# The first load of a row-mean kernel, issued as two transfers: partitions 0 to 15, then 16 to 127

## The chip, the cores and the metric

One core of one Trainium2 chip. The time is the device time of the core in microseconds (us), as a median over several executions.

Some terms: data comes from HBM (67.11 MB read, by the page of before) into SBUF, where a tile of this kernel has 128 partitions (128x14336 in the reductions). DMA engines move it: the packet records of before fall into sixteen strings, taken here as one per engine. A packet is one such record, here the rows of one load for one partition (57,344 B for 14 rows). A transfer is issued by one instruction and has landed when all its packets are written.

## The reference

```python
batch, seq, dim = 32, 512, 1024
def reference(x, divisor):           # x: (32, 512, 1024) float32, divisor 1024.0
    return (np.sum(x, axis=-1) / divisor).astype(np.float32)
```

There are 16,384 rows of 4 KB, 67.1 MB in all, each summed to one number. The work is to read everything once.

## The kernel before

Each of the 128 partitions gets 128 rows. A load takes some rows of every partition; VectorE sums them with one reduction per load, ScalarE helps at the end. All loads go through one queue (issued by SyncE), into three large buffers of 14 rows, and the first three are issued before anything else runs.

```python
first = [(2, 0), (14, 0)]                            # (rows, of these on ScalarE)
main = [(14, 0)] * 5 + [(14, 4), (12, 5)]
last = [(9, 4), (4, 2), (2, 1)]
...
for loads, src, dst in ((first, x_first, res0), (main, x_main, res)):
    j = 0
    for rows, on_act in loads:
        t = bulk.tile([P, 14, D], F32, name="t")     # three buffers
        load(t[:, :rows, :], src[:, j : j + rows, :])
        d = rows - on_act
        ...                                          # ScalarE sums rows d to rows-1
        nc.vector.reduce_sum(out=dst[:, j : j + d], in_=t[:, :d, :], axis=AX)
        j += rows
    nc.gpsimd.tensor_scalar_mul(out=dst, in0=dst, scalar1=scale)
...                                                  # the last 16 rows, in ever smaller loads: t, t4, t2, pa, pb
```

Of the kernel before, what the change touches and what calls it, by code (L numbers as in the profile page):

```python
# [125 lines left out]
@with_exitstack  # L126
def kernel(
    ctx: ExitStack,
    tc: tile.TileContext,
    x: bass.AP,  # L130
    divisor: float,
    out: bass.AP,
):
    nc = tc.nc
    landed = nc.alloc_semaphore("landed")
    nc.at_finalize(start_loads_at_once)
    nc.at_finalize(latest_wait_first)
    nc.at_finalize(lambda nc: close_while_storing(nc, landed))
    xf = x.flatten_outer_dims()
    N, D = xf.shape  # L140
    P = nc.NUM_PARTITIONS
    scale = 1.0 / float(divisor)
    J = N // P
    assert J * P == N


    F, L = 16, 16
    M = J - F - L
    W = M + L
    x_first = bass.AP(tensor=x.tensor, offset=0, ap=[[F * D, P], [D, F], [1, D]])  # L150
    x_main = bass.AP(tensor=x.tensor, offset=P * F * D, ap=[[W * D, P], [D, M], [1, D]])
    x_last = bass.AP(tensor=x.tensor, offset=P * F * D + M * D, ap=[[W * D, P], [D, L], [1, D]])
    o_first = bass.AP(tensor=out.tensor, offset=0, ap=[[F, P], [1, F]])
    o_main = bass.AP(tensor=out.tensor, offset=P * F, ap=[[W, P], [1, M]])
    o_last = bass.AP(tensor=out.tensor, offset=P * F + M, ap=[[W, P], [1, L]])


    first = [(2, 0), (14, 0)]
    main = [(14, 0)] * 5 + [(14, 4), (12, 5)]
    last = [(9, 4), (4, 2), (2, 1)]  # L160
    assert sum(n for n, _ in first) == F
    assert sum(n for n, _ in main) == M and sum(n for n, _ in last) == L - 1

    pad = ctx.enter_context(tc.tile_pool(name="pad", bufs=1))
    pad.tile([P, 224], F32, name="pad")
    bulk = ctx.enter_context(tc.tile_pool(name="bulk", bufs=3))
    one = ctx.enter_context(tc.tile_pool(name="one", bufs=1))
    psum = ctx.enter_context(tc.tile_pool(name="junk", bufs=4, space=bass.MemoryType.PSUM))


    c = 512
    t4 = one.tile([P, 4, D], F32, name="t4")
    t2 = one.tile([P, 2, D], F32, name="t2")
    pa = one.tile([P, 768], F32, name="pa")[:, :c]
    pb = one.tile([P, D - c + 16], F32, name="pb")[:, : D - c + 2]
    res0 = one.tile([P, F], F32, name="res0")
    res = one.tile([P, M], F32, name="res")
    fin = one.tile([P, L], F32, name="fin")
    nc.gpsimd.memset(pb[:, D - c :], 0.0)  # L179

    def load(dst, src):
        tc.keep_in_program_order(nc.sync.dma_start(out=dst, in_=src))  # L182

    def act_sum(dst, src, by=1.0):
        junk = psum.tile([P, D], F32, name="junk")
        nc.scalar.activation(junk, src, COPY, scale=by, accum_out=dst)  # L186

    def dve_mean(dst, src, by=scale):


        h = src.shape[-1] // 2
        nc.vector.tensor_tensor_reduce(  # L192
            out=src[:, :h], in0=src[:, :h], in1=src[:, h:], scale=by, scalar=0.0,
            op0=ADD, op1=ADD, accum_out=dst,
        )

    for loads, src, dst in ((first, x_first, res0), (main, x_main, res)):
        j = 0
        for rows, on_act in loads:
            t = bulk.tile([P, 14, D], F32, name="t")  # L200
            load(t[:, :rows, :], src[:, j : j + rows, :])
            d = rows - on_act
            for i in range(d, rows):
                act_sum(dst[:, j + i : j + i + 1], t[:, i, :])
# [4 lines that stand above are left out]
    for rows, on_act in last:  # L209
        t = bulk.tile([P, 14, D], F32, name="t")[:, :rows, :] if rows > 4 else t4 if rows == 4 else t2  # L210
        load(t, x_last[:, j : j + rows, :])
        d = rows - on_act
        for i in range(rows):
            if i < d:
                dve_mean(fin[:, j + i : j + i + 1], t[:, i, :])
            else:
                act_sum(fin[:, j + i : j + i + 1], t[:, i, :], by=scale)
        j += rows
    load(pa, x_last[:, j, :c])
    load(pb[:, : D - c], x_last[:, j, c:])  # L220


    tc.keep_in_program_order(nc.sync.dma_start(out=o_first, in_=res0))
    tc.keep_in_program_order(nc.sync.dma_start(out=o_main, in_=res))

    dve_mean(pb[:, D - c : D - c + 1], pa, by=1.0)
    dve_mean(fin[:, j:], pb)
    tc.keep_in_program_order(nc.sync.dma_start(out=o_last, in_=fin))
# [35 lines left out]
```

## Time and profile before

| | before |
|---|---|
| time | 160.38 us, median of 3 (160.35 to 160.44) |
| span of the profile | 159.0 us |
| VectorE busy | 117.2 us |
| DMA, mean over the span | 422 GB/s |
| a 57,344 B packet (14 rows), start to start on one DMA engine | 2.113 us, 27.1 GB/s |
| an 8,192 B packet (the first load's 2 rows) | 0.306 us |
| first load landed, first reduction starts | 4.63 us |
| last load (pb) landed | 157.08 us |

The prediction below shows the lines and works them out.

### The profile page before, as it was taken

The numbers are of one execution on the slowest core, as the hardware profiler recorded it, in microseconds if no ns is written. First come the engines' busy times: TensorE is split into PE (matmuls) and PEld (weight loads), VectorE is DVE, ScalarE is ACT, GpSimd is POOL, SyncE is SP. The second block draws the span as 40 slices with busy tenths as digits, with TensorE's granted clock in tenths as the row PEclk, the third lists the DMA queues.
The fourth block names the chain that finished last, engine by engine and source line by source line (L and its number), as shares of the span: only waits on it lengthen the run. The fifth ranks groups of instructions, "written<-read, shape, count | busy, mean of one in ns | idle before, by whom it ended". The sixth has DMA issues, their size and how long they took to land.

```text
span 159.0 us, 148 instructions
## 1 busy us (share of the span) xinstructions
DVE 117.2 (74%) x29; ACT 18.5 (12%) x33; POOL 1.0 (1%) x7
## 2 busy tenths in 40 slices
DVE  0500059995999599978999599959995996395643
ACT  3000000000000000000000000000000900390684
POOL 0000000000000000000000000000000000001000
DMA  7999999959999999699999999699999999999894
GB/s 278 447 462 462 462 462 462 462 260 433 462 462 462 462 462 462 303 390 462 462 462 462 462 462 404 303 447 462 462 462 429 396 396 408 482 445 445 350 420 169
DMA packets 2448, 67.18 MB, mean 422 GB/s; under 512 B 656, under 2 KB 656, under 8 KB 912
## 3 DMA queue, kind: packets, MB, share of 16 engines
q1 hardware_dynamic: 2448, 67.18, 98.3%
HBM read 67.11 MB, written 0.07 MB: 422 GB/s over the span
## 4 chain that ended last, share of the span: by engine, by line
DMA 77%; DVE 21%; SPq 1%; issue 0%; DVEq 0%
DMA t<-in_x_dram 56%; DMA pb<-in_x_dram 21%; DVE res L205 20%; SPq L182 1%; DVE pb L192 0%; DVEq L259 0%
## 5 line engine op out<-in xcount | busy, mean ns | idle before, releaser
L205 DVE TENSOR_REDUCE res<-t 128x14 f32<-128x14336 f32 (+3 forms) x9 | 111.2, 12360 | 34.0 <-DMA t<-in_x_dram 34.0
L186 ACT ACTIVATE junk<-t 128x1024 f32<-128x1024 f32 x16 | 16.2, 1013 | 136.8 <-DMA t<-in_x_dram 136.8
L192 DVE CUSTOM_DVE_ANT_0 t<-t 128x512 f32<-128x512 f32 x8 | 5.1, 688 | 6.1 <-DMA t<-in_x_dram 6.1
L186 ACT ACTIVATION_READ_ACCUMULATOR junk<-t 128x1 f32 x16 | 3.0, 186 | 0.0
L207 POOL TENSOR_SCALAR res<-res 128x16 f32<-128x16 f32 (+1 forms) x2 | 0.7, 352 | 143.3 <-DVE res L205 143.3
L186 ACT ACT_TABLE_LOAD x1 | 1.3, 1283 | 1.7 <-PEq L245 1.7
L192 DVE DVE_READ_ACCUMULATOR2_ANT fin<- 128x1 f32 x9 | 0.7, 82 | 0.0
L192 DVE CUSTOM_DVE_ANT_0 pb<-pb 128x257 f32<-128x257 f32 x1 | 0.4, 428 | 0.2 <-DMA pb<-in_x_dram 0.2
L192 DVE CUSTOM_DVE_ANT_0 pa<-pa 128x256 f32<-128x256 f32 x1 | 0.4, 426 | 0.0
L179 POOL MEMSET pb<- 128x2 f32 x1 | 0.1, 99 | 1.3 <-POOLq L245 1.3
L245 POOL MEMSET const-bfloat16-1.0<- 128x1 bf16 x1 | 0.1, 101 | 0.0
L245 POOL MEMSET const-uint8-127<- 128x1 uint8 x1 | 0.1, 101 | 0.0
L245 POOL MEMSET const-float32-0.0<- 128x1 f32 x1 | 0.1, 98 | 0.2 <-issue 0.2
L245 POOL MEMSET const-float32-1.0<- 128x1 f32 x1 | 0.1, 98 | 0.0
L192 DVE DVE_READ_ACCUMULATOR2_ANT pb<- 128x1 f32 x1 | 0.1, 84 | 0.0
## 6 DMA issues: line engine op xcount, KB each, us to landing
t<-in_x_dram SPq DMA_DIRECT2D x7, 7168.0 KB, 35.6
t<-in_x_dram SPq DMA_DIRECT2D x1, 6144.0 KB, 33.3
t<-in_x_dram SPq DMA_DIRECT2D x1, 4608.0 KB, 27.2
t<-in_x_dram SPq DMA_DIRECT2D x2, 1024.0 KB, 19.2
t<-in_x_dram SPq DMA_DIRECT2D x1, 2048.0 KB, 31.7
pa<-in_x_dram SPq DMA_DIRECT2D x1, 256.0 KB, 33.8
pb<-in_x_dram SPq DMA_DIRECT2D x1, 256.0 KB, 33.9
out_dram<-res SPq DMA_DIRECT2D x1, 48.0 KB, 11.6
```

The source lines that it names most:

```text
L179: nc.gpsimd.memset(pb[:, D - c :], 0.0)
L182: tc.keep_in_program_order(nc.sync.dma_start(out=dst, in_=src))
L186: nc.scalar.activation(junk, src, COPY, scale=by, accum_out=dst)
L192: nc.vector.tensor_tensor_reduce(out=src[:, :h], in0=src[:, :h], in1=src[:, h:], scale=by, scalar=0.0, op0=ADD, op1=ADD, accum_out=dst,)
L205: nc.vector.reduce_sum(out=dst[:, j : j + d], in_=t[:, :d, :], axis=AX)
L207: nc.gpsimd.tensor_scalar_mul(out=dst, in0=dst, scalar1=scale)
L245: nc = _bacc.Bacc("TRN2", target_bir_lowering=False, num_devices=1)
```

## The change

The intent is to give every DMA engine its first packet sooner: the first issue covers only 16 partitions, one row pair for each of the 16 engines, and the other 112 partitions follow.

```diff
         for rows, on_act in loads:
             t = bulk.tile([P, 14, D], F32, name="t")
-            load(t[:, :rows, :], src[:, j : j + rows, :])
+            if rows == 2:
+
+                load(t[:16, :rows, :], src[:16, j : j + rows, :])
+                load(t[16:, :rows, :], src[16:, j : j + rows, :])
+            else:
+                load(t[:, :rows, :], src[:, j : j + rows, :])
```

## The prediction

> **What bounds the kernel now.** I read the page's first two parts, then the chain of waits, the waits of the load queue, the order in time of the first microseconds, and at last the trace's single DMA packets. The page:
>
> ```profile
> DVE 117.2 (74%) x29; ACT 18.5 (12%) x33; POOL 1.0 (1%) x7
> ...
> DMA  7999999959999999699999999699999999999894
> GB/s 278 447 462 462 462 462 462 462 260 433 462 462 462 462 462 462 303 390 462 462 462 462 462 462 404 303 447 462 462 462 429 396 396 408 482 445 445 350 420 169
> ...
> DMA 77%; DVE 21%; SPq 1%; issue 0%; DVEq 0%
> ```
>
> The DMA row is at 9 from the second slice to the end; the dips (5, 6) are slices that fall between the starts of large packets, not pauses, as the packets below show. The chain gives 21% to DVE, which would make VectorE a second bound. The order of time shows why it is not one:
>
> ```profile
> 4.63 2.29 DVE L205 TENSOR_REDUCE res<-t 128x2 f32<-128x2048 f32 x1 [4.63 <-DMA t<-in_x_dram]
> 21.51 15.09 DVE L205 TENSOR_REDUCE res<-t 128x14 f32<-128x14336 f32 x1 [14.59 <-DMA t<-in_x_dram]
> ...
> 38.44 15.09 DVE L205 TENSOR_REDUCE res<-t 128x14 f32<-128x14336 f32 x1 [1.84 <-DMA t<-in_x_dram]
> 55.42 15.09 DVE L205 TENSOR_REDUCE res<-t 128x14 f32<-128x14336 f32 x1 [1.89 <-DMA t<-in_x_dram]
> ```
>
> Each 14-row reduction lasts 15.09 us and the loads land 16.9 us apart (38.44 to 55.42): VectorE waits 1.8 us each time, so the loads are the bound. The chain passes through VectorE only because a later load is issued when a buffer comes free. That issue is early enough: the third buffer is refilled at 6.95 us, and by then the ring holds two 14-row loads, enough until 38.4. The last link of the chain is the last load, pb, and 0.43 us of VectorE:
>
> ```profile
> 123.14 33.94 DMA pb<-in_x_dram
> 157.08 0.02 issue
> 157.10 0.43 DVE pb L192
> ```
>
> The single packets in the trace can be strung together per DMA engine, since the next starts within some nanoseconds of the last one's end. Sixteen strings come out. A packet of 57,344 B (14 rows) takes 2.113 us from start to start, which is 27.1 GB/s for an engine and 434 for sixteen; one of 8,192 B (the first load's rows) takes 0.306 us. The first load is eight such packets on each engine. All sixteen first packets start between 1.02 and 1.68 us; most last 0.3 to 1.0 us instead of 0.31, and nearly all end at about 2.0. From there every string runs without a pause to the last microsecond. The first load's strings end at 3.87 to 4.28 us, and the same spread of 0.4 us is still there at 150 us. So **an engine that loses time in the first 4 us never makes it up, and the slowest of the sixteen sets the end**. That gives the sum: 1.70 us until data flows (2.0 less one packet of 0.306); 4.19 MB per engine at 27.1 GB/s, 154.6 us; some 0.7 for the smaller packets, the completion writes and the spread; 2.0 from the last landing (157.08) to the end. It is 159.0, the span. The only thing that the change can move is the first term and what the two transfers do until their strings end.
>
> [...]
>
> **The change part by part.** *Removed:* one issue of 1 MB, eight descriptors for each engine. *Added:* an issue of 16 rows (128 KB, one descriptor each) and one of 112 rows (896 KB, seven each). Bytes and packets are the same; each engine gets one more completion write, some 6 ns from its start to the next packet's in the strings. *Moved:* the second transfer and all later ones are issued one place later. The first issue takes 0.383 us and the next two 0.43 each, so the 112 rows come at about 0.4, the 14-row loads at 0.85 and 1.3 in place of 0.43 and 0.91. Those are needed at 4 us, so that is hidden. On the engines nothing moves: the order of instructions per engine is the same but for the extra issue.
>
> *Gain.* If the first descriptor of an engine comes sooner[...], the first packets could all start at about 1.0 instead of 1.0 to 1.7. But that buys little: the ones that started early waited longest, and all ended at 2.0. Nor may the second transfer lag: it brings data some 0.4 us behind the first, while the first covers only 0.306. I take the gain as 0 to 0.2 us, and the lag as 0.1 (0.43 less 0.306) lost again. Net 0.
>
> *Loss.* The 16 rows go to partitions 0 to 15, [...] **+0.92 us on every engine**. Then come 112 rows. [...] The slowest counts[...]: +0.6 to +1.2, say 0.9. The sum is 0.92 + 0.9 = +1.8 us, which reaches the end in full, since strings don't catch up: 160.38 + 1.8 = 162.2.
>
> **The rivals.**
> - *A[...]* (above): 162.2 us. [...] Against: no line of before shows a collision. Chance 0.5.
> - *B, only the first transfer collides*[...]: +0.9 to +1.0, so 161.3. Chance 0.2.
> - *C, nothing collides*, [...] the wait for the first data at 1.0 to 2.0 us hides it: 160.2 to 160.5. The author's hope is the lower end. For it: 0.5 to 0.7 us of each first packet is latency. Chance 0.2.
> - *D, the rows of the second transfer are dealt out one by one*, so that sixteen neighbouring partitions are always written at once: [...] 8 x 0.92 = +7.3 us, 167.7 us. [...] Chance 0.08.
>
> A wait that takes the place of the removed one is not among them: the first reduction starts at 4.63 us and has 14.6 us of idle time behind it, so it may start at 6 us at no cost; the refill of its buffer moves from 6.95 to about 8.8, still 29 us ahead of need. The shift of the completion semaphores by one place makes later issues look at transfers that landed over 15 us earlier.
>
> **Range and chances.** The middle of A (162.2), B (161.3) and C (160.4), by their chances, is near 161.8 us, +0.9%. From 160.3 (C) to 163.0 (A with the worst engine at 1.7 instead of 0.9) holds eight times in ten. Slower by over 2% means 163.6 or more: D, and a thin tail of A, 0.09. Faster by over 2% would need 3.2 us, twice what lies before the first data: 0.01. Within 2%: 0.90.
>
> **What would show it.** In the changed profile: first packets that last 1.2 us or more in place of at most 1.0[...]; a spread of the ends of the first load's strings well over 0.4 us (collisions of the 112 rows); the first reduction later than 4.63, at 5.5 under B and 6 or more under A, and the last load's landing later than 157.08 by as much as the slowest string lost. VectorE's 15.09 us and the 16.9 us between landings stay. I am wrong if the first reduction starts at 4.7 us or sooner (C), if it is past 8 us (D), or if it is late and the end isn't, since then strings do catch up.

The marked cuts are passages on the hardware that no run of this case shows. The forecast's sum came to +1.8 us, 0.92 for the 16 rows and 0.9 for the 112, on 160.38 us: 162.2 us, the figure of rival A. Packets "collide" when they hold each other up: A has both transfers of the change collide, B the first alone, C neither, and D has each step of the second as slow as that of the 16 rows. The amounts of B and D use the same 0.92.

## The result, and the profile after

The changed kernel took 161.28 us (median of 4, one of them slow; its fast runs 161.11 to 161.37) against 160.41 us for before on the same chip. The ratio of the fast runs is 1.0052, 95% interval 1.0034 to 1.0069: 0.5% slower. Ratios here are the mean time of one kernel's fast runs over that of the other's fast runs in the same rounds, so they are not quite the ratio of the quoted medians.

The first profile of the changed kernel fell in the slow state, in which single executions of three of the kernels here took some 12 to 19 us longer than the others (179.72 us against 161.28; a 57,344 B packet lasted 2.38 us instead of 2.12), so it says nothing on a difference of 1 us. The kernel was run once more (run "again" below), and its fast profile, of a run of 161.27 us, is the one read here. First the page's busy rows, DMA rows and chain:

```profile
DVE 117.2 (73%) x29; ACT 18.5 (12%) x33; POOL 1.0 (1%) x7
...
DMA  7999879999999969999999969999999999999894
GB/s 207 514 459 459 359 330 459 459 459 459 459 459 459 402 287 459 459 459 459 459 459 459 416 272 459 459 459 459 459 459 426 393 393 393 492 443 443 344 422 168
...
DMA 77%; DVE 21%; SPq 1%; issue 0%; DVEq 0%
```

The shape is that of before: the same VectorE work, the same chain, a DMA row at 9 nearly throughout. Now the reductions in order of time (start, length, engine, and in brackets the idle time before it and what ended it):

```profile
6.05 2.29 DVE L210 TENSOR_REDUCE res<-t 128x2 f32<-128x2048 f32 x1 [6.05 <-DMA t<-in_x_dram]
22.74 15.09 DVE L210 TENSOR_REDUCE res<-t 128x14 f32<-128x14336 f32 x1 [14.40 <-DMA t<-in_x_dram]
39.61 15.09 DVE L210 TENSOR_REDUCE res<-t 128x14 f32<-128x14336 f32 x1 [1.78 <-DMA t<-in_x_dram]
56.51 15.09 DVE L210 TENSOR_REDUCE res<-t 128x14 f32<-128x14336 f32 x1 [1.81 <-DMA t<-in_x_dram]
```

The first reduction starts 1.42 us later than before (4.63), the third 1.17 later (38.44), the fourth 1.09 later (55.42), and the loads still land 16.9 us apart. The whole loss is there before 23 us. The last pieces of the chain show what is left of it:

```profile
124.06 33.95 DMA pb<-in_x_dram
158.01 0.02 issue
158.04 0.43 DVE pb L192
```

The last load lands at 158.01 instead of 157.08 us, 0.93 later, and the span is 159.9 instead of 159.0.

The issue rows of the two new transfers (KB, us from issue to landing):

```profile
t<-in_x_dram SPq DMA_DIRECT2D x1, 896.0 KB, 5.5
...
t<-in_x_dram SPq DMA_DIRECT2D x1, 128.0 KB, 2.7
```

The 128 KB of the 16 rows take 2.7 us to land, over half of the 4.6 us that all of the first load took in before. For the early microseconds the packet records were strung together per engine, as in the prediction. The records name no engine, so a string can change over to another where two packets end within nanoseconds of each other; averages over all sixteen don't depend on it. Typical strings (start, length in us; 8 KB packets, then 57,344 B ones):

```
before   1.027 0.869 | 1.893 0.309 | 2.199 0.309 | 2.505 0.309 | 2.811 0.309 | 3.117 0.309 | 3.423 0.309 | 3.729 0.309 | 57 KB: 4.040 2.116, 6.153 2.116
changed  1.040 0.521 | 1.564 1.055 | 2.615 0.309 | 2.921 0.309 | 3.227 0.436 | 3.660 0.392 | 4.048 0.408 | 4.453 0.480 | 57 KB: 4.935 2.354, 7.286 2.116
```

Three things differ. The first packet is through sooner (1.56 instead of 1.89), although the first packets start hardly 0.1 us sooner on the mean and the earliest at 1.02 in both. The second, the first of the 112 rows, then takes over a microsecond here and 0.92 on the mean. And the fifth to eighth packets take 0.39 to 0.48 us instead of 0.31, the first large one 2.35 instead of 2.12. From the second large packet on the two run alike. Its start, averaged over the sixteen engines, is the measure used from here on: 6.27 us in before, 7.32 in the changed kernel, **1.05 later**. (How far can one profile be trusted? Four runs below leave the first load whole, on four chips; their second large packet starts at 6.23 to 6.29.) At the 41st large packet of each engine it is 88.76 against 89.75, 0.99 later. Nothing is caught up beyond some hundredths.

### The profile page after: what moved, and what is told of

It reads as the page before. It is cut to its first block, busy times and chain, and to the rows that moved or that the text cites. A ratio compares the mean times of both kernels' runs of the same rounds, so it can differ in the third digit from the quotient of the medians.

```text
span 178.4 us, 150 instructions
## 1 busy us (share of the span) xinstructions
DVE 117.3 (66%) x29; ACT 18.5 (10%) x33; POOL 1.0 (1%) x7
## 4 chain that ended last, share of the span: by engine, by line
DMA 70%; DVE 26%; another core or an unknown queue 2%; SPq 2%; issue 0%; DVEq 0%
DMA t<-in_x_dram 47%; DVE res L210 25%; DMA pb<-in_x_dram 22%; SPq L182 2%; DVE pb L192 0%; DVEq L264 0%
```

## The experiments

The theories: **P**, the packets of a transfer to only part of the 128 partitions hold each other up (collide), and last longer than those of a transfer to all of them; **L**, the second transfer pays a wait of its own for first data, which one packet of the first transfer can't cover. The short first packets of the slow profile (0.35 to 0.58 us) had already spoken against the 1.2 us first packets of P.

### again: the changed kernel once more

> The changed kernel once more, because its only profile fell in the slow state (178.4 us span, a 57,344 B packet 2.378 us instead of 2.113). Theory P[...]: fast time 161.2 to 161.4, in the packet records either first packets of 1.2 us[...] or, since the slow profile already shows first packets of 0.35 to 0.58 us, packets of the 112 rows that last well over 0.31 us each on some engines. Theory L (the second transfer pays its own wait for first data): same time; first packets end by 1.4 to 1.8 us, the second packet of each engine ends at about 2.4 to 2.8 instead of 2.3, all later ones last 0.31 us, strings of the first load end 0.3 to 0.6 later than before.

161.34 us (161.13 to 161.89), before 160.50 in the same rounds, ratio 1.0058 (1.0039 to 1.0077). The strings above are from it. Both theories find their sign: L in the second packet (it ends at 2.4 to 2.9 us on the engines), P in the later packets above 0.31 us. The next runs part them.

### swap: the large part first

```diff
-                load(t[:16, :rows, :], src[:16, j : j + rows, :])
-                load(t[16:, :rows, :], src[16:, j : j + rows, :])
+                load(t[0:112, :rows, :], src[0:112, j : j + rows, :])
+                load(t[112:128, :rows, :], src[112:128, j : j + rows, :])
```

> First load as two transfers in the other order of sizes: partitions 0 to 111 first, 112 to 127 second. Theory P: the 112 rows still collide, so +0.6 to +1.0 us, about 161.2. Theory L: the first transfer has seven packets per engine (2.1 us), which covers the second's wait for data, so 160.3 to 160.6, like before.

161.58 us, ratio 1.0073 (1.0058 to 1.0088). Seven packets per engine of cover did not bring the time back to before, so L alone is out. The strings start like those of before (first packets end at 1.8 to 2.2), then go from 0.31 to about 0.40 us a packet by the fifth, and the large packet after the 16 rows takes 2.6 to 3.1 us in place of 2.1. The second large packet starts 1.25 us later than in before.

### cols: the split by columns, over all 128 partitions

```diff
-                load(t[:16, :rows, :], src[:16, j : j + rows, :])
-                load(t[16:, :rows, :], src[16:, j : j + rows, :])
+                flat = t.rearrange("p r d -> p (r d)")
+                for a, b in ((0, 256), (256, 2048)):
+                    load(flat[:, a:b], bass.AP(tensor=x.tensor, offset=a, ap=[[F * D, P], [1, b - a]]))
```

> First load as two transfers over all 128 partitions: 256 columns (8 KB per engine, as much cover as 16 rows), then 1792. [...] Theory P: 160.4, no loss (at most 0.1). Theory L: the loss stays, +0.5 to +0.9 us, 160.9 to 161.3.

160.77 us, ratio 1.0016 (0.9999 to 1.0033; each of its runs, from 160.73 up, lies above all seven of before, up to 160.56), and the second large packet starts 0.30 us late. Both theories missed: P expected no loss, L the whole of it. The same 8 KB per engine ahead of the rest cost a third of the change's loss. But for a few single packets, none later than the second transfer's first two is slow in these strings. This is the part that L explains.

### mid16 and mid7: the same split deep in the queue, and its control

A load with packets of 57,344 B should make a collision seven times as long, by an estimate from the lengths in before (2.113 us against 0.306), and with two loads queued ahead of it a wait for first data should not show. mid7 is the control for that.

```diff
-            load(t[:, :rows, :], src[:, j : j + rows, :])
+            if src is x_main and j == 14:                       # mid16
+                load(t[0:16, :rows, :], src[0:16, j : j + rows, :])
+                load(t[16:128, :rows, :], src[16:128, j : j + rows, :])
+            else:
+                load(t[:, :rows, :], src[:, j : j + rows, :])
```

```diff
+            if src is x_main and j == 14:                       # mid7
+                load(t[:, :7, :], src[:, j : j + 7, :])
+                load(t[:, 7:, :], src[:, j + 7 : j + 14, :])
```

> First load whole as before; the second 14-row main load, deep in the queue, split into partitions 0 to 15 and 16 to 127. Rows of 57,344 B make any collision seven times as long, and the queue hides any wait for first data. Theory P: [...] 166 to 172 us. Only the 112 rows colliding: 162.5 to 166. Theory L: 160.4 to 160.6.

> Control for mid16: the same middle load as two transfers, but both over all 128 partitions (7 rows each). [...] 160.4 to 160.7. If instead a second transfer deep in the queue costs time by itself: well above 161.

mid16 took 179.78 us, ratio 1.1204 (1.1187 to 1.1221): **19 us for one load split by partitions**, more than the expected 6 to 12. mid7 took 160.47 us, ratio 0.9984 (0.9965 to 1.0004): a second transfer cost nothing here, deep in the queue. The reductions of mid16 in order of time show where it is:

```profile
39.17 15.09 DVE L209 TENSOR_REDUCE res<-t 128x14 f32<-128x14336 f32 x1 [2.50 <-DMA t<-in_x_dram]
75.49 15.09 DVE L209 TENSOR_REDUCE res<-t 128x14 f32<-128x14336 f32 x1 [21.23 <-DMA t<-in_x_dram]
```

and those of mid7 for the same loads:

```profile
38.58 15.09 DVE L209 TENSOR_REDUCE res<-t 128x14 f32<-128x14336 f32 x1 [1.88 <-DMA t<-in_x_dram]
55.68 15.09 DVE L209 TENSOR_REDUCE res<-t 128x14 f32<-128x14336 f32 x1 [2.02 <-DMA t<-in_x_dram]
```

VectorE waits 21.23 us for the split load and 2.02 for the other. The busy time by stretch of mid16 (stretch and its length; busy us and number of instructions of VectorE, ScalarE and GpSimd; TensorE clock; DMA share; GB/s):

```profile
20.00:40.00 20.00, 15.91 (x2) 0.00 (x0) 0.26 (x1) 1.00 1.21 413
40.00:60.00 20.00, 14.26 (x1) 0.00 (x0) 0.00 (x0) 1.00 0.90 218
60.00:80.00 20.00, 4.51 (x1) 0.00 (x0) 0.00 (x0) 1.00 0.92 281
```

The DMA share stays at 0.90 and 0.92 while the rate falls to 218 and 281 GB/s; in before the same two stretches have shares of 1.05 and 0.95 at 453 and 413 GB/s. So here a "busy" DMA row did not tell a stream at full speed from one that was held up.

### mid64 and mid48: other places for the cut

The same edit as mid16, with the cut at partition 64 and at 48.

> The middle load of mid16 as two halves, partitions 0 to 63 and 64 to 127: [...] 8 x 2.11 = 16.9 us more: 177 to 178. [...]

> A test of the rule that the two middle splits gave[...]. Split at partition 48: shares of 3 rows, [...] (3 x 2.11 = 6.3 us a step), then shares of 5[...] (4.0 to 4.5 us). Sum 3 x 6.3 + 5 x 4.25 = 40 us for a load that takes 16.9: 183 us, 180 to 186. If the engines did not hold each other up[...]: 170 to 178.

mid64 took 179.03 us (median of 4, one slow; fast runs 178.93 to 179.09), ratio 1.1155, 18.5 us more than before where 16.9 was expected: above its range of 177 to 178. The reductions at its split load start 35.4 us apart (38.96 and 74.37), those of the same loads in before 17.0 (38.44 and 55.42). mid48 took 186.47 us (fast runs), ratio 1.1603, 25.9 us more where 23 was worked out, half a microsecond outside the expected range. Its profile fell in the slow state: large packets last 2.11 us before the split load and 2.37 after it. Its steps below, with the 2.80 us of the packet after them, exceed nine of 2.11 us by 26.2 us, close to the 25.9 of the fast runs, so they are hardly lengthened by it. The lengths of the steps, which are the differences between the mean starts of the engines' successive packets, 2.11 us each in before:

```
split  step lengths of the split load, us (the bar parts its two transfers)
mid16  7.18 | 4.64 4.13 2.89 3.21 4.01 4.14 4.03
mid64  3.89 4.48 4.48 4.49 | 4.25 4.48 4.48 4.49
mid48  6.12 7.24 7.24 | 4.52 4.29 4.36 4.33 4.32
```

Every step of a transfer to part of the partitions is longer than 2.11 us: 6.1 to 7.2 us with 16 and 48 partitions, 3.9 to 4.5 with 64, 4.3 to 4.5 with 80, 2.9 to 4.6 with 112. Which packets meet in each step no run shows, so what sets the length of a single step, and why two of mid16 are as short as 2.89 and 3.21, is not shown. The figures are means of all sixteen engines, and single packets in the middle of mid16 last 4.1 us on every engine. **The whole set of engines was slowed together.** In the shortest step (2.89) just two packets are slower than the rest: 4.05 and 4.03 us beside 2.54 to 2.98. The two strings that they belong to stay some 1.5 us behind, which accounts for most of the difference between the 19.3 us that mid16 lost at its end and 18.3 in the mean of the strings.

A rival is the reading side: a split by partitions changes also which addresses of HBM are read at once. No run tests it alone, so it is not shown on which side the packets are held up.

### half: the strong dose in the first load

```diff
+                load(t[0:64, :rows, :], src[0:64, j : j + rows, :])
+                load(t[64:128, :rows, :], src[64:128, j : j + rows, :])
```

> First load as partitions 0 to 63, then 64 to 127: [...] Theory P: up to 8 x 0.306 = 2.45 us more in the strings, of which the wait for first data may hide up to 0.9: 161.9 to 163.1. Theory L alone (second transfer's wait for data; four packets per engine, 1.2 us, cover it): 160.4 to 160.7.

162.80 us, ratio 1.0128 (1.0108 to 1.0148). The second large packet starts 2.39 us late, beside 2.45 for eight doubled steps of 0.306. Some 0.3 of it is no collision: in this profile the first issue took 0.56 us instead of 0.38, and the first packet started at 1.34 instead of 1.02. The first two reductions:

```profile
7.50 2.29 DVE L209 TENSOR_REDUCE res<-t 128x2 f32<-128x2048 f32 x1 [7.50 <-DMA t<-in_x_dram]
24.21 15.09 DVE L209 TENSOR_REDUCE res<-t 128x14 f32<-128x14336 f32 x1 [14.42 <-DMA t<-in_x_dram]
```

The second starts 2.70 us after that of before. With its later packets at 0.5 to 0.65 us instead of 0.31, P acts in the first load too.

### extra16 and extra128: the 16 rows by themselves

The first load is left whole; an extra transfer of 128 KB goes ahead of it, into a tile that is overwritten at the end.

```diff
+            if rows == 2:
+                load(t2[:16, :, :], src[:16, j : j + rows, :])       # extra16
+                load(t2[:, 0, :256], src[:, j, :256])                # extra128, in its place
             load(t[:, :rows, :], src[:, j : j + rows, :])
```

> Control for extra16: the first load whole as before, with an extra transfer ahead of it, 256 columns over all 128 partitions (8 KB per engine) into a tile that is overwritten later. It adds 0.31 us of bytes and the second transfer's wait (0.3 us in the column split), no collision: 160.9 to 161.2, first strings 0.5 to 0.7 us later than before.

> The same extra bytes as 16 rows on partitions 0 to 15[...], followed by the whole first load[...]. The difference from extra128 is the collision of the 16 rows by itself. If that is paid in full: +0.9 us over extra128. If it passes beneath the second transfer's wait for data: 0 to 0.3 over extra128, and then the loss of the changed kernel beyond the wait is the 112 rows'.

extra128 took 161.01 us, ratio 1.0032 (1.0017 to 1.0047); extra16 161.23, ratio 1.0048 (1.0031 to 1.0065). The intervals overlap, and the second large packet starts at 6.83 and 6.87 us. Yet the 16 rows do collide. The issue rows (KB, us from issue to landing) of the extra transfer, first in extra128 and then in extra16:

```profile
t<-in_x_dram SPq DMA_DIRECT2D x1, 128.0 KB, 2.2
```

```profile
t<-in_x_dram SPq DMA_DIRECT2D x1, 128.0 KB, 2.9
```

The same bytes land 0.7 us later on 16 partitions than on 128. The whole first load behind them is not later by more than 0.04 us in the strings, probably because it waits for its own first data in that time; that is the author's reading. (The last completion record of the 16 rows is at 1.66 us, 1.2 us before they land; in the changed kernel it is at 1.70 and they land at 2.7, a gap of 1.0; in extra128 the gap is 0.4 and in before 0.33. So for the 16 rows the last record lies 0.7 to 0.9 us further ahead of the landing than for a transfer to all 128 partitions.)

### row1 and cut512: can the early data be had without the loss?

The column split with other cuts: at 1024 (one row each) and at 512.

> First load as two transfers of one row over all 128 partitions (eight packets of 4 KB per engine each, 1.2 us of cover[...]). Theory P alone: no loss, 160.4 to 160.6. Theory L: the cover reaches past the second transfer's wait, so no bubble, and the smaller first packets bring the first data sooner: 160.1 to 160.5. If two transfers cost time whatever their form: 160.7 or more, like the column split.

> Column split at 512 in place of 256 (16 KB per engine, 0.6 us of cover). Theory L: the bubble of the 256-column split (+0.27 us) shrinks by the 0.3 us of added cover, 160.3 to 160.6. If the loss of the 256-column split was not the second transfer's wait but the price of one more transfer: 160.7 to 160.9.

cut512: 160.57 us, ratio 1.0002 (0.9974 to 1.0030), the second large packet 0.09 us late. Doubling the first transfer's bytes took the lateness from 0.30 to 0.09, as L has it; this rests on one profile each, since the interval of the times takes in the ratio of cols. row1: 160.96 us, ratio 1.0013 (0.9996 to 1.0031; before was unsteady in these rounds, 160.39 to 161.20), 0.42 us late in the strings. L expected less. Its strings show no long wait where the second transfer begins but a second set of slow packets (0.2 to 0.5 us in place of 0.16) between 3.0 and 3.9 us, which neither theory has. Its time fits the third outcome, a price of two transfers in any form, but cut512 speaks against that one. It stays open. No form of the split beat the single transfer.

### All of them in one table

Lateness is the mean start of the second large packet less 6.27 us, from one profile each; the last column is the difference of the medians in the same rounds.

| kernel | lateness, us | time less before, us |
|---|---|---|
| cut512 | 0.09 | -0.04 |
| cols | 0.30 | 0.27 |
| row1 | 0.42 | 0.35 |
| extra128 | 0.56 | 0.52 |
| extra16 | 0.60 | 0.74 |
| again (the change) | 1.05 | 0.84 |
| swap | 1.25 | 1.08 |
| half | 2.39 | 2.19 |

What is lost before 7 us is lost at the end, within 0.25 us, in every row.

## Why the prediction was right or wrong

**The range and the class held**: 161.28 lies between 160.3 and 163.0, and the kernel is within 2%. The point, 161.8, was 0.5 us too high, and its sum was put together from terms that are wrong one by one: 0.92 for the 16 rows, 0.9 for the 112 and 0 for the wait came out as 0.04 (0.2 by the medians), 0.6 to 0.75 and 0.3. So it was right that both transfers are slower on their partitions than one over all 128, and that what reaches the large packets is lost to the end, but that the range held owes something to luck.

- *The bound, and that strings don't catch up*: right. 1.05 us at the second large packet, 0.99 at the 41st, 0.84 in the medians; the table shows it for eight kernels. The refill of the buffer, the semaphores and VectorE's idle time stayed out of it, as said.
- *"+0.92 us on every engine"* for the 16 rows: they are slower, as said, but the place on the path is wrong. In mid16 their step took 7.18 us instead of 2.11; in the changed kernel the 16 rows landed 2.7 us after their issue, where the same bytes over 128 partitions needed 2.2 in cols. But extra16 against extra128 puts what reaches the end at 0.04 us by the strings and 0.2 by the medians. The prediction took wait and collision as things to add; the runs fit the two lying side by side.
- *"Net 0"* for gain and lag: wrong. The first packets are through about 0.4 us sooner (their ends average 1.60 us instead of about 2.0), as the change hoped, but the second transfer's first data come only at 2.4 to 2.9 us. The prediction gave that lag as 0.1 us, from the distance of two issues. What it costs, measured without any collision (cols), is 0.30 in the strings and 0.27 in the time.
- *The 112 rows, "+0.6 to +1.2, say 0.9"*: what is left of 1.05 after 0.30 is 0.75 us, less at most 0.05 of the 16 rows; in the medians 0.84 less 0.27, 0.57. This is the largest term. The changed kernel's own packets give the same parts: on the mean its second packets end 0.32 us later than those of before (2.61 against 2.29), and the other 0.74 is lost after them. The working behind the term let the slowest engine count, and all sixteen went slowly together, but for two strings of mid16.
- *Rivals*: B's figure, 161.3, is the one that came out, by luck: it has the 16 rows cost 0.9 us and the 112 nothing, and it was nearly the other way round. C was right that a wait for first data hides a collision, if the reading of extra16 above holds, and that of the 16 rows only. D would have made every step of mid16 as long as its first (7.18 us), and only the first was; the others took 2.89 to 4.64.
- *The signs to look for*: first packets of 1.2 us did not come (0.52 us in the string above, and they end at 1.60 on the mean), perhaps since the last record of the 16 rows lies 1.0 us ahead of their landing; a wider spread of the string ends did not come either (0.42 us, as before), since the engines are slow together. The first reduction at 6 us did come.
- *Slips that change nothing*: A, B and C weighted by their chances give 161.6, not 161.8. And C's "0.5 to 0.7 us of each first packet": in the records of before the first packets last 0.43 to 1.01 us, 0.12 to 0.70 more than the later ones (0.309), 0.47 on the mean.

Two sizes stay open. Scaled from mid16 (27.05 us for the seven steps less 14.8, divided by 7) the 112 rows should cost 1.75 us on 8 KB rows, and cost 0.6 to 0.75: the second and third of the seven still take only 0.32 and 0.35 us on the mean. Why the short packets lose less than the scaled amount, no run shows. Nor does a run show why a second transfer waits for data that long.

## What to carry to other kernels

Where DMA engines streamed without a pause to the end, as here, what was lost in the first load came out at the end within 0.25 us, so look at the packets there and not at the share of busy time, which was 0.90 at 218 GB/s in mid16 and 1.05 at 453 in before. Split such a transfer by its rows or columns rather than by partitions: on a middle load a split by rows cost nothing (160.47 us) and one by partitions 19 us (179.78); on the first load splits by columns or rows came 0.09 to 0.42 us late and splits by partitions 1.05 to 2.39. A small transfer sent ahead was late unless it covered the wait of the next: by columns, with 8 KB per engine the lateness was 0.30 us, with 16 KB 0.09, and neither gained anything.
